# A decoder trunk's two mixers: part of the weight splitting moved from VectorE to GpSimd, one job ahead of its products

## The chip, the cores and the metric

The kernel runs on one core of one Trainium2 chip. The metric is the device time of one execution in microseconds (us); the time before is the median of three runs. The core's engines are called by the names of the profile: PE (TensorE, the matrix products), PEld (its weight loads), DVE (VectorE), ACT (ScalarE), POOL (GpSimd) and SP (SyncE, whose queue issues the loads). Each engine works through its own queue of instructions in a fixed order and waits at an instruction until what that instruction needs is there.

## The reference, cut to what matters

A trunk of two layers on 256 tokens of width 1024. Layer 0 has a hybrid mixer (four heads of a gated delta rule and four heads of block attention, side by side), layer 1 an attention mixer with low-rank queries and keys (MLA). After each mixer comes a feed-forward layer of 16384 single-neuron experts.

```
for layer in range(DEPTH):
    mod = cond @ mod_w[layer] + mod_b[layer]
    sh1, sc1, g1, sh2, sc2, g2 = jnp.split(mod[:, None, :], 6, axis=-1)
    h = rmsnorm(x, norm_mix[layer]) * (1.0 + sc1) + sh1
    if layer % 2 == 0:
        y = hybrid_mixer(h, ...)      # h @ w_in, delta rule and block attention, @ w_out
    else:
        y = mla_mixer(h, ...)         # h @ w_in, @ w_uq, @ w_ukv, attention, @ w_out
    x = x + g1 * y
    h = rmsnorm(x, norm_ffn[layer]) * (1.0 + sc2) + sh2
    x = x + g2 * peer_ffn(h, ...)
return rmsnorm(x, final_norm)
```

In the delta rule, each chunk of 64 tokens needs the inverse of a unit lower triangular matrix, a chain of small products; `o_a = rmsnorm(o_a, o_norm) * silu(z_a)` closes it, and `z_a` is one more part of `h @ w_in`.

## The kernel before, in words

All products are in fp32 accuracy from a faster number form, fp32r: each operand is split into a part `hi` and a rest `lo`, and `mm3` (lines 134 to 138) makes three matrix products of them, hi by hi (L136), hi by lo or lo by hi (L137, L138). `split` (L130 to L132) makes the two parts: the cast to `hi` on ACT, the subtraction of `hi` from the source on DVE. Both appear in the profile under L132.

**Weights in the mixers.** A weight chunk of 128x2048 (1 MB) is loaded into `wraw` (two buffers) and split by `fetch` in two pieces of 128x1024 into `whi` and `wlo` (three buffers each in the hybrid mixer, two in the MLA mixer). `drive` runs over a list of jobs, one for each chunk and block of products. In each of the two halves of a job it emits some of the job's products, then one piece of the split of a chunk that comes one job (MLA) or two jobs (hybrid) later, and then a step of each of the other chains of work: the delta rule's gates, its triangular inverse and its state, the rotary embedding, the attention and the modulation of the next sub-layer (`mod`, L349, two 128x1024 products with a sum on DVE for each 1 MB of its weights).

**What sets the order.** In the mixers a scheduler orders the instructions of each engine by its own estimates of when they are ready; the written order is only its start. So another engine or another duration for one instruction can change where others stand, on PE, DVE, ACT and SP alike. Within the expert layers the order is the written one. GpSimd's own work in the mixers is small: it multiplies two 128x512 tiles (L1169) and one (L1287) in the delta rule, and four 128x256 tiles for `silu(z_a)` (L1357).

**Names near the change.** `wlo_...` are the split chunks, with a running number. In the hybrid mixer the delta rule's gates go through L1051 to L1073 to the products L1069 and L1088; the scaled keys through L1166 and L1168 to L1177 (the triangle `F`), whose last write is the zeroing of a quarter, L1180; L868 are PE transposes of `F`, and the inverse starts from them (L1190, L1200, L1210, L1212). At the mixer's end L1309 and L1310 are the last state products, L1313 to L1325 scale, norm and gate the result `F` on DVE, L875 transposes it on PE, and the products with `w_out` follow. In the MLA mixer `ckT` is the normed latent, from which keys and values are made.

Of the kernel before, what the change touches and what calls it, by code (L numbers as in the profile page):

```python
# [9 lines left out]
F32 = mybir.dt.float32  # L10
# [57 lines left out]
class Trunk:  # L68
# [58 lines left out]
        nc.vector.memset(self.eps, RS * EPS / 4)  # L127


    def split(self, hi, lo, src):  # L130

        return self.nc.scalar.copy(hi, src), self.nc.vector.tensor_sub(lo, src, hi.bitcast(F32))  # L132

    def mm3(self, out, l, r, start, stop):
        mm = self.nc.tensor.matmul
# [647 lines left out]
        self.nc.sync.dma_start(raw[:, :w], src)  # L783
        return raw

    def fetch(self, src, kt, n, pieces=2, raw=None, parts=None):

        w = kt * n
        raw = self.load(src, w) if raw is None else raw
        hi, lo = parts or (self.t(self.wp, [P, WMAX], F32R, tag=t, bufs=self.sets) for t in ("whi", "wlo"))  # L790
        steps = [lambda c=slice(k * w // pieces, (k + 1) * w // pieces): self.split(hi[:, c], lo[:, c], raw[:, c])
                 for k in range(pieces)]
        return Parts(kt, n, [hi[:, :w]], [lo[:, :w]]), steps

    def weights(self, src, kt, n, raw=None):
# [5 lines left out]
    def drive(self, jobs, chains, early=()):  # L801

        self.later = []
        early = list(early)
        ws = []

        def get():  # L810
            if len(ws) < len(jobs):
                w = early.pop(0) if early else None
                ws.append(w if isinstance(w, tuple) else self.fetch(*jobs[len(ws)][0], raw=w))
        ahead = self.sets - 1
        for _ in range(ahead):
            get()
        for w, steps in ws:
            while steps:
                steps.pop(0)()
        for j in range(len(jobs)):  # L820
            get()
            steps = ws[j + ahead][1] if j + ahead < len(jobs) else []
            if len(jobs[j]) > 2:
                jobs[j][2]()
            g = jobs[j][1](ws[j][0])
            for half in range(2):
                late, self.later = self.later, []
                next(g, None)
                if steps:
                    steps.pop(0)()  # L830
                for f in late:
                    f()
                for c in list(chains):
                    if next(c, chains) is chains:
                        chains.remove(c)
            for _ in g:
                pass
            while steps:
                steps.pop(0)()
# [1041 lines left out]
```

## Time and profile before

| | |
|---|---|
| time before, median of 3 runs | 1913.13 us (1910.81 to 1915.3) |
| time of the profiled execution | 1913.58 us |
| its span in the trace | 1911.8 us |
| mean granted TensorE clock | 0.997 of full speed |
| PE busy | 1878.6 us (98%) |
| DVE busy | 1532.3 us (80%) |
| ACT busy | 943.5 us (49%) |
| POOL busy | 48.9 us (3%) |

The hybrid mixer lies at about 45 to 205 us, the MLA mixer at about 995 to 1110 us; the rest is the conditioning at the start and the two expert layers. A row of a timeline gives the start, the duration, the engine, the line, the operation with its tiles, and in brackets how long the engine stood idle before it and which instruction ended that. A matmul's duration overlaps the next one's: what it costs PE is the step from start to start.

### The profile page before, as it was taken

The page shows a single profiled execution, that of the slowest core. Times are in us where ns is not written, and L with a number is a line of the kernel's source. Part 1 is how long each engine was busy: PE and PEld are TensorE (multiplying, and loading weights), DVE is VectorE, ACT ScalarE, POOL GpSimd, SP SyncE. Part 2 cuts the span into 40 slices and gives each one's busy share as a digit, 9 for nine tenths or more (in the row PEclk, how much of TensorE's full clock was granted, in tenths as well). Part 3 has the DMA queues.
Part 4 walks back from the last instruction along what each step waited for, and adds up shares of the span by engine and source line. Part 5 has one row for each costly group of instructions (what it writes and reads, how often), then busy time and mean ns, then how long its engine had stood idle before and what let it go on. Part 6 is the DMA issues. An engine that isn't in the chain of part 4 may idle for free.

```text
span 1911.8 us, 35995 instructions
## 1 busy us (share of the span) xinstructions
PE 1878.6 (98%) x14368; PEld 1722.2 (90%) x14368; DVE 1532.3 (80%) x3265; ACT 943.5 (49%) x1301; POOL 48.9 (3%) x131
## 2 busy tenths in 40 slices
PE   6999999999999999999999999999999999999998
PEld 6999899999999888888889899999999988888886
DVE  7879789999998789865657677999778878985565
ACT  2866555454444444454545754545444444444453
POOL 7001000000000000000000000000000000000000
PEclk9999999999999999999999999999999999999999
DMA  8456475658885555576743455565555555556673
GB/s 324 160 194 214 191 279 187 201 187 284 295 270 187 177 177 177 176 251 195 216 147 111 155 201 175 183 203 186 180 175 170 176 177 176 176 180 199 194 228 103
DMA packets 96504, 374.57 MB, mean 196 GB/s; under 512 B 11856, under 2 KB 12112, under 8 KB 89680
## 3 DMA queue, kind: packets, MB, share of 16 engines
q1 hardware_dynamic: 96336, 372.28, 58.4%
q8 instruction: 112, 1.84, 0.4%
q14 instruction: 56, 0.46, 0.1%
HBM read 371.18 MB, written 1.05 MB: 195 GB/s over the span
## 4 chain that ended last, share of the span: by engine, by line
PE 82%; DVE 9%; DMA 4%; ACT 3%; issue 1%; SPq 0%; ACTq 0%; DVEq 0%
PE ps L776 30%; PE ps L621 21%; PE ps L623 11%; PE ps L136 3%; PE ps L138 3%; PE ps L137 3%; PE ps L644 3%; DVE lo L132 3%; DMA raw<-in_v_dram 2%; PE ps L729 1%; DVE t L349 1%; PE ps L324 1%; ACT hi L132 1%; PE ps L1200 1%; DVE wlo L132 1%
## 5 line engine op out<-in xcount | busy, mean ns | idle before, releaser
L132 ACT CAST hi<-raw 128x1024 fp32r<-128x1024 f32 x508 | 534.8, 1054 | 753.1 <-PE ps L776 310.5
L132 DVE TENSOR_TENSOR lo<-raw,hi 128x1024 fp32r<-128x1024 f32 x508 | 620.0, 1222 | 249.0 <-ACT hi L132 246.8
L621 PE MATMUL ps<-hT,hi 128*128 128x256 f32 x4096 | 514.2, 278 | 0.0
L621 PEld LDWEIGHTS ps<-hT,hi 128*128 128x128 f32 x4096 | 485.8, 188 | 0.2 <-ACT hi L132 0.2
L623 PE MATMUL ps<-hT,lo 128*128 128x256 f32 x2048 | 276.7, 278 | 2.0 <-DVE lo L132 1.9
L776 PE MATMUL ps<-hi,vwh 128*128 128x512 f32 x976 | 266.1, 394 | 1.2 <-ACT hi L132 1.1
L776 PE MATMUL ps<-hi,vwl 128*128 128x512 f32 x976 | 261.3, 389 | 0.0
L776 PE MATMUL ps<-lo,vwh 128*128 128x512 f32 x976 | 260.9, 389 | 0.0
L623 PEld LDWEIGHTS ps<-hT,lo 128*128 128x128 f32 x2048 | 252.4, 188 | 4.1 <-DVE lo L132 3.7
L776 PEld LDWEIGHTS ps<-hi,vwl 128*128 128x128 f32 x976 | 183.2, 188 | 38.8
L776 PEld LDWEIGHTS ps<-lo,vwh 128*128 128x128 f32 x976 | 183.2, 188 | 38.3
L776 PEld LDWEIGHTS ps<-hi,vwh 128*128 128x128 f32 x976 | 180.3, 188 | 38.1 <-ACT hi L132 2.9
L132 DVE TENSOR_TENSOR wlo<-wraw,whi 128x1024 fp32r<-128x1024 f32 (+1 forms) x84 | 99.3, 1202 | 36.1 <-ACT whi L132 36.0
L132 ACT CAST whi<-wraw 128x1024 fp32r<-128x1024 f32 (+1 forms) x84 | 84.3, 1032 | 36.5 <-PE ps L137 14.2
L640 DVE TENSOR_TENSOR ohG<-ohB,t 128x512 f16<-128x512 f16 x256 | 99.3, 418 | 0.0
L136 PE MATMUL ps<-hT,whi 128*128 128x256 f32 x288 | 85.0, 296 | 7.1 <-ACT hT L247 7.1
L634 DVE TENSOR_TENSOR ohA<-t,t 128x1024 f16<-128x1024 f16 x128 | 87.6, 684 | 0.0
L137 PE MATMUL ps<-hT,whi 128*128 128x256 f32 x288 | 83.1, 289 | 0.2 <-DVE hT L251 0.2
L138 PE MATMUL ps<-hT,wlo 128*128 128x256 f32 x288 | 83.1, 289 | 0.0
L644 PE MATMUL ps<-ohG,ohA 128*128 128x64 f16 x2048 | 79.0, 193 | 0.3
L644 PEld LDWEIGHTS <-ohA 128*128 128x128 f16 x2048 | 67.3, 97 | 12.2 <-issue 8.7
L349 DVE SCALAR_TENSOR_TENSOR t<-t,t 128x1024 f32<-128x1024 f32 x56 | 67.4, 1217 | 2.5 <-DMA t<-in_modT_dram 2.5
(478 smaller groups left out, 2251.7 us busy)
## 6 DMA issues: line engine op xcount, KB each, us to landing
raw<-in_uT_dram SPq DMA_DIRECT2D x256, 512.0 KB, 3.3
raw<-in_v_dram SPq DMA_DIRECT2D x256, 512.0 KB, 4.1
t<-in_modT_dram SPq DMA_DIRECT2D x56, 512.0 KB, 5.0
wraw<-in_w_dram SPq DMA_DIRECT2D x13, 1024.0 KB, 6.0
raw<-in_modT_dram SPq DMA_DIRECT2D x24, 512.0 KB, 4.4
wraw<-in_wq_dram SPq DMA_DIRECT2D x12, 1024.0 KB, 5.7
mw<-in_mod_dram SPq DMA_DIRECT2D x8, 1024.0 KB, 13.6
wraw<-in_w0start_dram SPq DMA_DIRECT2D x4, 1024.0 KB, 12.0
```

Of the source, the lines that this page charges most:

```text
L132: return self.nc.scalar.copy(hi, src), self.nc.vector.tensor_sub(lo, src, hi.bitcast(F32))
L136: mm(out, l[0], r[0], start=start, stop=False)
L137: mm(out, l[0], r[1], start=False, stop=False)
L138: mm(out, l[1], r[0], start=False, stop=stop)
L324: mm(ps[g][:, i], e.hT[:, s, k, sl], w[:, b, k, :], start=s + k + b == 0, stop=s == 1 and n == KD - 1)
L349: self.nc.vector.scalar_tensor_tensor(w, w, 1.0, self.row, op0=OP.mult, op1=OP.mult, accum_out=self.modc[layer][:, c:c + 1])
L621: mm(pair, hi[:, k], hT[:, s, k], start=k == 0 and s == 0, stop=False)
L623: mm(pair, lo[:, k], hT[:, 0, k], start=False, stop=k == KD - 1)
L634: nc.vector.tensor_tensor(A, self.iota_t[:, None].to_broadcast(full), pairs(0, full), op=OP.is_equal)
L640: nc.vector.tensor_tensor(B[:, j], b0, pairs(2 + j, part), op=OP.mult)
L644: nc.tensor.matmul(ps[:, t], A[:, t // 2, :, t % 2], B[:, j, t // 2, :, t % 2], start=j == 0, stop=j == 1)
L776: self.nc.tensor.matmul(acc[i][c], w[a][:, j, i * P:(i + 1) * P], v[b][:, c * 512:(c + 1) * 512], start=first and j + a + b == 0, stop=False)
```

## The change

`split` and `fetch` take an engine for the subtraction. `fetch` gives it to the last of its pieces only, and `drive` asks for GpSimd in the chunks that it fetches itself. Chunks that are fetched before `drive`, and the queries' weights, stay wholly on DVE. So 12 chunks of the hybrid mixer and 9 of the MLA mixer have the `lo` part of their second half, 128x1024 each, subtracted on GpSimd: 21 of the 84 subtractions `wlo`. The cast to `whi` stays on ACT.

```diff
-    def split(self, hi, lo, src):
+    def split(self, hi, lo, src, engine=None):
 
-        return self.nc.scalar.copy(hi, src), self.nc.vector.tensor_sub(lo, src, hi.bitcast(F32))
+        return self.nc.scalar.copy(hi, src), (engine or self.nc.vector).tensor_sub(lo, src, hi.bitcast(F32))
...
-    def fetch(self, src, kt, n, pieces=2, raw=None, parts=None):
+    def fetch(self, src, kt, n, pieces=2, raw=None, parts=None, engine=None):
...
-        steps = [lambda c=slice(k * w // pieces, (k + 1) * w // pieces): self.split(hi[:, c], lo[:, c], raw[:, c])
-                 for k in range(pieces)]
+        steps = [lambda c=slice(k * w // pieces, (k + 1) * w // pieces), v=(None, engine)[k == pieces - 1]:
+                 self.split(hi[:, c], lo[:, c], raw[:, c], v) for k in range(pieces)]
...
-                ws.append(w if isinstance(w, tuple) else self.fetch(*jobs[len(ws)][0], raw=w))
+                ws.append(w if isinstance(w, tuple) else self.fetch(*jobs[len(ws)][0], raw=w, engine=self.nc.gpsimd))
```

The scheduler then places the mixers' instructions anew. On GpSimd, at the end of the hybrid mixer, the subtractions come in between the products of `silu(z_a)` (L1357, tile `t_568`) that the result's gate L1325 on DVE needs:

```order
 L1357 TENSOR_TENSOR t_568<-t_568,t_102 128x256
 L1287 TENSOR_TENSOR t_733<-qkv_560,t_733 128x512
-L1357 TENSOR_TENSOR t_568<-t_568,t_102 128x256 x3
+L1357 TENSOR_TENSOR t_568<-t_568,t_102 128x256
+L132 TENSOR_TENSOR wlo_2082<-wraw_2079,whi_2081 128x1024
+L1357 TENSOR_TENSOR t_568<-t_568,t_102 128x256 x2
+L132 TENSOR_TENSOR wlo_2162<-wraw_2159,whi_2161 128x1024
+L132 TENSOR_TENSOR wlo_2196<-wraw_2193,whi_2195 128x1024
```

The third and fourth L1357 now stand behind the second half of `wlo_2082`.

On DVE, where the delta rule's triangle is made (some 80 to 92 us before): the piece from the scaling of the keys (L1166) to the zeroing of the first triangle's quarter (L1180), `F_898`.

```order
 L1166 TENSOR_TENSOR t_730<-t_730,ps_902 128x512
-L922 TENSOR_TENSOR ropf_166_1005<-ps_979,t_100 128x128
+L349 SCALAR_TENSOR_TENSOR raw_1229,t_86<-raw_1229,t_88 128x1024
 L1168 TENSOR_TENSOR k_154_908<-t_730,t_728 128x512
-L923 TENSOR_TENSOR lo_741<-rope_165_1004,ropf_166_1005 128x2x64
+L1166 TENSOR_TENSOR t_731<-t_731,ps_954 128x512
 L1177 SCALAR_TENSOR_TENSOR F_898<-ps_911,t_892,k_154_908 128x128 x4
-L924 TENSOR_TENSOR rope_165_1004<-ps_979,t_100 128x128
-L925 TENSOR_TENSOR ropf_166_1005<-ps_979,t_100 128x128
-L1166 TENSOR_TENSOR t_731<-t_731,ps_954 128x512
-L926 TENSOR_TENSOR lo_741<-rope_165_1004,ropf_166_1005 128x2x64
-L1180 MEMSET F_898 64x4x64
```

Small rotary steps have left the piece and a 128x1024 modulation product (L349) has come in; another L349 comes in just ahead of the piece (behind the step L1149), and a third between the piece and the zeroing of the second triangle. All three stood behind both triangles before.

On PE, at the end of the hybrid mixer, the transposes L875 of the gated result `F_2030` stood before behind the `w_out` products of four accumulators, `ps_2163`, `ps_2178` (not shown), `ps_2197` (not shown) and `ps_2212`:

```order
L138 MATMUL ps_2212<-whi_2081,qkT_1869 128x512
L136 MATMUL ps_2212<-whi_2081,qkT_1869 128x512
L137 MATMUL ps_2212<-wlo_2082,qkT_1869 128x512
L875 MATMUL ps_2145<-t_76,F_2030 128x128 x4
L875 MATMUL ps_2152<-t_76,F_2030 128x128 x4
```

and stand now behind those of the first alone:

```order
L138 MATMUL ps_2163<-whi_1900,qkT_1869 128x512
L136 MATMUL ps_2163<-whi_1900,qkT_1869 128x512
L137 MATMUL ps_2163<-wlo_1901,qkT_1869 128x512
L875 MATMUL ps_2145<-t_76,F_2030 128x128 x4
L138 MATMUL ps_2163<-whi_1900,qkT_1869 128x512
L875 MATMUL ps_2152<-t_76,F_2030 128x128 x4
L136 MATMUL ps_2178<-whi_1900,qkT_1869 128x512
```

L875 has moved ahead of 36 products of 128x512. On DVE the gate L1325 has moved too: it stands now ahead of both first halves of the last two chunks (`wlo_2162`, `wlo_2196`), of which it had three pieces ahead of it.

## Rows read from the trace of the kernel before

**Rows 1.** The page, part 1 (busy time of each engine) and part 4 (the chain).

```profile
PE 1878.6 (98%) x14368; PEld 1722.2 (90%) x14368; DVE 1532.3 (80%) x3265; ACT 943.5 (49%) x1301; POOL 48.9 (3%) x131
...
PE 82%; DVE 9%; DMA 4%; ACT 3%; issue 1%; SPq 0%; ACTq 0%; DVEq 0%
```

**Rows 2.** The page, part 5: the subtractions, the modulation; busy, mean ns | idle before.

```profile
L132 DVE TENSOR_TENSOR wlo<-wraw,whi 128x1024 fp32r<-128x1024 f32 (+1 forms) x84 | 99.3, 1202 | 36.1 <-ACT whi L132 36.0
...
L349 DVE SCALAR_TENSOR_TENSOR t<-t,t 128x1024 f32<-128x1024 f32 x56 | 67.4, 1217 | 2.5 <-DMA t<-in_modT_dram 2.5
```

**Rows 3.** Stretches of 20 us: busy time (instructions) of each engine, PEclk, DMA share.

```profile
50.00:70.00 20.00, 19.26 (x147) 18.36 (x146) 16.98 (x45) 18.35 (x35) 0.00 (x0) 0.88 0.64 222
70.00:90.00 20.00, 19.90 (x163) 19.52 (x163) 16.77 (x59) 13.40 (x26) 2.58 (x2) 0.95 0.43 147
...
190.00:210.00 20.00, 19.36 (x94) 15.17 (x93) 17.76 (x46) 7.58 (x21) 0.77 (x17) 1.00 0.55 209
...
1020.00:1040.00 20.00, 18.90 (x158) 18.18 (x157) 17.08 (x58) 12.31 (x24) 0.00 (x0) 1.00 0.59 209
```

**Rows 4.** Timeline of POOL in the hybrid mixer: start, duration, [idle before <-releaser].

```profile
83.07 1.28 POOL L1169 TENSOR_TENSOR t<-t,t 128x512 f32<-128x512 f32 x1 [35.15 <-issue]
...
168.59 0.74 POOL L1357 TENSOR_TENSOR t<-t,t 128x256 f32<-128x256 f32 x1 [79.63 <-ACT t L1356]
170.48 1.46 POOL L1287 TENSOR_TENSOR t<-qkv,t 128x512 f32<-128x512 f32 x1 [1.15 <-ACT qkv L1116]
...
181.30 1.10 POOL L1357 TENSOR_TENSOR t<-t,t 128x256 f32<-128x256 f32 x1 [5.52 <-ACT t L1356]
```

**Rows 5.** Timeline of DVE beside those POOL instructions.

```profile
170.73 2.29 DVE L349 SCALAR_TENSOR_TENSOR raw<-raw,t 128x1024 f32<-128x1024 f32 x1
...
176.87 0.15 DVE L182 TENSOR_TENSOR rs_4t<-rs_4t,rs_4v 128x8 f32<-128x8 f32 x1
...
181.74 0.68 DVE L182 TENSOR_TENSOR rs_4t<-rs_4t,rs_4v 128x8 f32<-128x8 f32 x1
```

**Rows 6.** Timeline of DVE, from the gates to the second triangle's end.

```profile
76.51 0.17 DVE L1071 COPY t<-ps 128x8 f32<-128x8 f32 x1 [0.56 <-PE ps L1069]
...
91.60 0.27 DVE L1180 MEMSET F<- 64x256 f32 x1 [0.59 <-ACT t L1179]
```

**Rows 7.** Timeline of PE: the second triangle's transposes, and two products at full clock.

```profile
71.95 0.28 PE L136 MATMUL ps<-whi,hT 128*128 128x256 f32 x1
72.07 0.28 PE L137 MATMUL ps<-wlo,hT 128*128 128x256 f32 x1
...
91.93 0.66 PE L868 MATMUL ps<-t,F 128*128 128x128 f32 x4
```

**Rows 8.** Timeline of PE, end of the hybrid mixer.

```profile
179.35 0.39 PE L1310 MATMUL ps<-k,F 128*128 128x128 f32 x2
...
193.83 0.39 PE L136 MATMUL ps<-whi,qkT 128*128 128x512 f32 x1
194.06 0.39 PE L137 MATMUL ps<-wlo,qkT 128*128 128x512 f32 x1
194.93 1.23 PE L875 MATMUL ps<-t,F 128*128 128x128 f32 x8 [0.48 <-DVE F L1325]
```

**Rows 9.** Timeline of DVE there.

```profile
194.10 1.29 DVE L1325 TENSOR_TENSOR F<-F,t 128x512 f32<-128x512 f32 x2
```

**Rows 10.** Timeline of PE: the wait that precedes the slow clock.

```profile
64.57 0.28 PE L1035 MATMUL ps<-t,k 8*128 8x8 f32 x2 [0.74 <-ACT k L1031]
```

**Rows 11.** Timeline of PE, DVE and ACT, each apart, in the MLA mixer.

```profile
1032.69 0.51 PE L136 MATMUL ps<-ckT,whi 128*128 128x256 f32 x2 [0.82 <-ACT ckT L132]
...
1102.80 0.39 PE L137 MATMUL ps<-wlo,qn 128*128 128x512 f32 x1
...
1026.98 1.22 DVE L132 TENSOR_TENSOR wlo<-wraw,whi 128x1024 fp32r<-128x1024 f32 x1
...
1098.56 2.00 ACT L132 CAST whi<-wraw 128x1024 fp32r<-128x1024 f32 x2 [2.16 <-PE ps L138]
```

## The prediction

> **What bounds the kernel now.** I read the busy times and the chain first. PE is busy for 1878.6 us of the 1911.8, and the chain of work that ended last is PE for 82% and DVE for 9% [rows 1]. So PE sets the time, and DVE counts only where PE stands waiting for it. Next I read the stretches of the two mixers, since nothing else changes its order. In the hybrid mixer PE is busy for 19.90 of 20 us at 70 to 90 us and for 19.36 of 20 at 190 to 210 us; the worst stretch of the MLA mixer has 18.90 of 20 [rows 3]. DVE is busy for 16.8 to 17.8 us of those same stretches, close to PE but below it. The reader is to see two things here. There is little to win: idle PE in the stretches shown, past the one at 50 to 70 us where no moved subtraction runs yet, sums to 0.10 + 0.64 + 1.10 us. And PE has almost no slack anywhere: whatever comes later than PE's fixed order expects is paid in full.
>
> **What is removed.** 21 subtractions of 1.20 us each leave DVE [rows 2], 25 us in all, 12 in the hybrid mixer (14.4 us) and 9 in the MLA mixer (10.8 us). None of this is on PE's path except at the waits for DVE named below. So removing it is worth at most those waits.
>
> **What is added.** GpSimd gets the same 21. The trace has no 128x1024 subtraction on it. The nearest rows are 0.74 us for 128x256 and 1.28 us for 128x512 [rows 4], that is 0.54 us for 256 more elements, so I take 1.28 + 2 x 0.54 = 2.4 us; from below 1.8 us (half that slope beyond 512 elements, 1.28 + 0.54), from above 2.9 us (twice the 1.46 of L1287). GpSimd itself has room, 48.9 us of work in 1911.8 [rows 1]. What counts is what it does to DVE. While GpSimd's L1287 ran from 170.48 for 1.46 us, DVE's L349 that started at 170.73 took 2.29 us [rows 4, 5] instead of its mean of 1.22 [rows 2]; it ended 1.07 us late, about what GpSimd still had to do (to 171.94). An L182 of 128x8 took 0.68 us beside GpSimd's L1357 at 181.30, which ended at 182.40, instead of 0.15 [rows 4, 5]. Both have two operands in SBUF. So a moved subtraction takes 1.2 us off DVE, and can stop DVE for up to 2.4 us when DVE comes to such an operation meanwhile. Subtractions `wlo`, L349, L1168, L1321 and L1325 are all of this kind. If about half the moved ones meet one near their start, DVE gains nothing on average. The Trainium skill (SBUF — State Buffer, Who interferes with whom) speaks against the change here: a DVE instruction with two SBUF inputs contends with a GpSimd instruction that reads SBUF, and the one that issues first holds the shared ports for its whole duration. The trace agrees, with 1.07 us lost by one L349 [rows 4, 5]; without the rule I would put the sum below about 1 us lower.
>
> **What is moved: the triangles (70 to 95 us).** In the new order L868 of the second triangle stands behind 10 products of 128x256 fewer, which step at 0.12 us [rows 7]: PE comes to it 1.2 us earlier. On DVE between L1071 and the second L1180, 15.1 us before [rows 6], three L349 come in (3 x 1.22 = 3.7 us) and one second half `wlo` goes out (1.2). Two convolution steps, three rotary steps net and some small ones go out as well; by their size against L349 I put these at 2 us. That is 0.5 us more, of which DVE's own waits there (0.59 us at its end alone [rows 6]) can take up as much, so -1 to +0.7. Two GpSimd subtractions and two L1169 lie in the stretch; a lock on one of the three L349 costs up to 2.4 us, on two 4.8. PE's stall is 1.2 + (-1 to +0.7) + (0 to 4.8): 0.2 to 6.7 us. I take 1.8, the case of one short lock, as in the row seen (1.07), with DVE's waits taking up part.
>
> **The end (180 to 200 us).** Before, L875 waited 0.48 us for L1325 [rows 8], and the products behind it a few tenths more: 0.8 us that may vanish. Now L875 stands ahead of 36 products of 128x512, 36 x 0.23 = 8.3 us earlier [rows 8]. Between the last L1310 and L875 there stand 40 products of 128x256 and 11 of 128x512: 40 x 0.12 + 11 x 0.23 = 7.3 us. DVE needs, from the first L1313: four pairs of 128x512 (L1313, L1316, L1321, L1325) of 1.29 us [rows 9], three pieces `dead` at 0.65 (half of such a pair) and nine small operations of 0.15 to 0.2 us: 5.2 + 2.0 + 1.6 = 8.8 us. It can begin about 1 us after L1310, since a first half `wlo_2082` and one `dead` still stand ahead. That is 9.8 us against 7.3, a stall of 2.5 us; by 1.5 us less, if DVE has run ahead through its relief, and up to 5 us more, if the second half of `wlo_2082` on GpSimd (2.4 us) and the two L1357 behind it hold L1321 or L1325. I take 2.6 - 0.8 = 1.8 us, bounds 0.2 to 6.7.
>
> **The rest of the hybrid mixer.** The gates at 70 to 77 us are small operations with two SBUF inputs under the first two GpSimd subtractions; I take 0.3 us (0 to 2). Between 95 and 165 us the modulation moved forward leaves DVE less to do, and PE is held there by nothing of DVE's: 0, up to 1.
>
> **The MLA mixer.** PE waited 0.82 us for `ckT` [rows 11]. One second half `wlo`, 1.22 us at 1026.98, stood on DVE ahead of it and now goes; GpSimd takes it up beside small operations. I take -0.7 us (-1.1 to +0.5). At the end, the last chunk's `whi` is cast by 1100.56 [rows 11]; GpSimd's 2.4 us then end at 1103.0, while the first product of that half with `wlo` starts at 1102.80 [rows 11]: +0.2 us (0 to 0.8). That is -0.5 in all. `wraw` comes free about 1 us later for each chunk and SP's queue, with the modulation loads behind it, waits for GpSimd too; no row of this mixer or the hybrid one shows PE waiting for a load of weights near its end, so nothing.
>
> **The sum.** 1.8 + 1.8 + 0.3 - 0.5 = +3.4 us. On the profiled execution's own time, 1913.58 us (1.8 us outside its span), it gives 1917.0 us. That execution is 0.45 us above the median of the runs, so I forecast 1916.5 us.
>
> **Rivals.** *The cover holds.* The scheduler put L875 and the triangles earlier by its own reckoning; if DVE really is ahead by the five to six subtractions moved before each place, the stalls stay under 0.5 us each and the waits of 0.8 and 0.7 us go. That gives -1.5 to +1.5 us, 1911.6 to 1914.6. For it: DVE's 16.8 of 20 us [rows 3] leave room for a delay to be caught up. Against it: the order on PE moved forward by more than one subtraction is worth.
>
> *The lock, with the clock.* In the row at 64.57 PE waited 0.74 us behind tiny products [rows 10], and the granted clock was 0.88 over 50 to 70 us and 0.95 over 70 to 90 us [rows 3], the lower of the two levels (1.2 GHz) for part of it. This cost 20 x 0.12 + 20 x 0.05 = 3.4 us. The clock did not fall at the MLA mixer's 0.82 us wait, where it stayed 1.00 [rows 3, 11]. The place where this can come again is L875 at the end: if GpSimd's `wlo_2082` and the L1357 behind it hold L1325, the stall is 5 us instead of 2.5. [...] The sum is then 3.4 + 2.5 + 3.4 = +9.3, 1922.4 us (1920 to 1926).
>
> *Faster.* All waits of PE for DVE vanish and the new order stalls nowhere: 0.8 + 0.7 us and the tenths at L868 give -2 us, not over 0.2%. To exceed 3.8 us the slow stretch at 65 us would have to end sooner, but it comes before the first moved subtraction. A price of 1907 to 1911 us, mostly by chance of the clock.
>
> *The change does nothing.* GpSimd's subtractions could end later than their products in general. But the pieces are split one or two jobs ahead, and a job of the hybrid mixer takes about 9 us (18 jobs in some 160 us); only the last chunk of the MLA mixer is near, as priced.
>
> **How the numbers follow.** The measurement of this kernel can tell about 0.2%, 3.8 us, from no change: below 1909.3 is faster, above 1917.0 slower. The forecast's case (1914.6 to 1920) gets 0.50, nearly half of it above 1917.0; the cover holds 0.30; the lock with the clock 0.14; faster 0.06. So slower 0.24 + 0.14 = 0.38, faster 0.05, same 0.57. The range from 1911.2 to 1923.0 takes in the first two cases and most of the third.
>
> **What would show it.** The subtractions on GpSimd at 2.2 to 2.6 us; DVE operations with two SBUF inputs (L349, L1168, L1321) of 2 us and more beside them; PE waiting 1 us or more at L868 for L1180 and at L875 for L1325; 0.5 us or less at `ckT`. It is wrong if the GpSimd subtraction takes 1.8 us or less, if PE's waits at L868 and L875 together stay under 1 us, or if PE loses time at a place not named, such as the inverse's products (L1200, L1210) or a load.

## The result and the profile after

The changed kernel takes 1931.66 us (median of 4 runs, 1929.1 to 1933.32) beside 1912.26 us for the kernel before on the same chip: a ratio of 1.0098 with a 95% interval of 1.0081 to 1.0116, slower by about 19 us. The forecast was 1916.5 us, with a range up to 1923.0. The profiled execution took 1931.4 us, its span 1929.6, 17.8 us more than before.

The first lines to set against [rows 1] are the busy times of the page of the changed kernel:

```profile
PE 1881.3 (97%) x14368; PEld 1723.6 (89%) x14368; DVE 1535.6 (80%) x3244; ACT 942.9 (49%) x1301; POOL 104.3 (5%) x152
```

DVE has 21 instructions fewer, which had taken 21 x 1.20 = 25.2 us [rows 2], and yet it is busy for 3.3 us more. So the instructions that stayed on DVE take some 28 us longer than they did. PE does the same 14368 products with 2.7 us more of busy time; the other 15.1 of the 17.8 us are idle time of PE. The first product of the first expert layer (L621) starts at 275.4 us instead of 263.9: 11.5 us are lost by the end of the hybrid mixer, and the other 6.3 us in the MLA mixer. The stretches of the changed kernel, in the columns of [rows 3], show where:

```profile
50.00:70.00 20.00, 19.34 (x142) 18.44 (x141) 17.21 (x45) 17.77 (x33) 0.54 (x1) 0.85 0.68 238
70.00:90.00 20.00, 16.30 (x135) 15.79 (x134) 19.41 (x50) 10.99 (x22) 9.50 (x5) 0.98 0.52 185
...
190.00:210.00 20.00, 15.62 (x66) 12.58 (x65) 14.74 (x23) 5.43 (x7) 5.79 (x3) 0.91 0.44 168
...
1060.00:1080.00 20.00, 18.04 (x133) 17.31 (x132) 8.90 (x15) 12.63 (x24) 4.87 (x2) 0.91 0.35 131
```

At 70 to 90 us PE falls from 19.90 to 16.30 us while DVE rises from 16.77 to 19.41: DVE is now the one that is waited for. At 190 to 210 us PE has 15.62 instead of 19.36 us. The granted clock has a new dip there (0.91, before 1.00), and another at 1060 to 1080 us. Before, the same stretch of time had the full clock:

```profile
1060.00:1080.00 20.00, 19.34 (x146) 18.10 (x145) 11.23 (x20) 15.27 (x40) 0.00 (x0) 1.00 0.35 131
```

Most of the cause stands in the timelines of POOL and DVE, here at four places of the changed kernel (start, duration; POOL's row first, then DVE's):

```profile
69.46 2.73 POOL L132 TENSOR_TENSOR wlo<-wraw,whi 128x1024 fp32r<-128x1024 f32 x1 [19.60 <-ACT whi L132]
...
85.40 2.38 POOL L132 TENSOR_TENSOR wlo<-wraw,whi 128x1024 fp32r<-128x1024 f32 x1 [0.32 <-ACT whi L132]
...
192.49 2.58 POOL L132 TENSOR_TENSOR wlo<-wraw,whi 128x1024 fp32r<-128x1024 f32 x1 [1.17 <-ACT whi L132]
...
1063.81 2.50 POOL L132 TENSOR_TENSOR wlo<-wraw,whi 128x1024 fp32r<-128x1024 f32 x1 [6.85 <-ACT whi L132]
...
69.86 2.35 DVE L1058 TENSOR_TENSOR t<-t,t 128x8 f32<-128x8 f32 x1
...
85.60 2.73 DVE L1168 TENSOR_TENSOR k<-t,t 128x512 f32<-128x512 f32 x1
...
192.18 3.44 DVE L1321 TENSOR_TENSOR F<-F,t 128x512 f32<-128x512 f32 x2
...
1064.01 2.44 DVE L926 TENSOR_TENSOR qr<-rope,ropf 128x128 f32<-128x128 f32 x1
```

The subtraction takes 2.4 to 2.7 us on GpSimd. L1058 works on 128x8 elements; [rows 5] has 0.15 us for another operation of that size. It starts 0.40 us after GpSimd and ends at 72.21, GpSimd at 72.19. L1168, of 128x512 elements, would take half of the pair in [rows 9], some 0.65 us; it ends at 88.33, 0.55 us after GpSimd's end at 87.78: it began its work when GpSimd had ended. The pair L1321 takes 3.44 us instead of the 1.29 of the like pair in [rows 9]. By comparing each DVE instruction beside a GpSimd subtraction with the usual duration of its form, 17 of the 21 subtractions stop one DVE instruction each, for 0.3 to 2.2 us, 26.7 us in all. The other four stop none: beside them DVE is idle (one), takes no second operand from SBUF (two), or had started first (one, where GpSimd took 2.94 us).

PE's waits of the changed kernel that answer to [rows 7, 8, 11], and those at new places:

```profile
80.01 0.41 PE L1164 MATMUL ps<-t,t 128*128 128x128 f32 x2 [1.84 <-DVE t L1149]
...
88.86 0.52 PE L868 MATMUL ps<-t,F 128*128 128x128 f32 x3 [1.76 <-DVE F L1180]
...
163.55 0.38 PE L1277 MATMUL ps<-k,k 128*128 128x128 f32 x1 [1.48 <-ACT k L1272]
...
196.28 0.66 PE L875 MATMUL ps<-t,F 128*128 128x128 f32 x4 [4.38 <-DVE F L1325]
...
199.07 0.63 PE L136 MATMUL ps<-whi,qkT 128*128 128x512 f32 x1
199.50 0.63 PE L137 MATMUL ps<-wlo,qkT 128*128 128x512 f32 x1
...
1040.94 0.30 PE L1464 MATMUL ps<-t,lat 128*128 128x128 f32 x1 [0.96 <-DVE lat L1458]
...
1066.51 0.55 PE L868 MATMUL ps<-t,qr 128*128 128x128 f32 x3 [1.96 <-DVE qr L926]
...
1100.99 0.33 PE L868 MATMUL ps<-t,att_s 128*128 128x128 f32 x1 [1.73 <-ACT att_s L949]
```

These seven waits sum to 14.1 us. The last of them, for `att_s`, is not made by a stop of DVE, since the two subtractions ahead of it (1083.00 and 1090.25) stop nothing there. The rows of POOL, SP and ACT ahead of it, and last the cast on ACT as it was before:

```profile
1090.25 2.35 POOL L132 TENSOR_TENSOR wlo<-wraw,whi 128x1024 fp32r<-128x1024 f32 x1 [4.88 <-ACT whi L132]
...
1092.62 0.33 SPq L783 DMA_DIRECT2D wraw<-in_w1out_dram  x1
...
1099.39 1.04 ACT L132 CAST hi<-raw 128x1024 fp32r<-128x1024 f32 x1 [2.36 <-DMA raw<-in_wq_dram]
1100.34 0.50 ACT L949 ACTIVATE att_s<-att_s,att_c 128x256 f32<-128x256 f32 x1
...
1082.72 1.05 ACT L132 CAST hi<-raw 128x1024 fp32r<-128x1024 f32 x1 [1.26 <-DMA raw<-in_wq_dram]
```

The subtraction reads `wraw` until 1092.60. Only then can SP issue the next load into this buffer (1092.62), and the load of the expert layer's weights `raw` stands behind it in SP's queue. ACT waits for that load 2.36 us at its cast, before 1.26, and the `att_s` that PE needs stands behind the cast in ACT's queue. After the longest wait, products of 128x512 step at 0.43 us instead of 0.23 [rows 8]: the lower of the two levels of the clock (1.2 GHz). By the stretches, 20 x 0.09 us at 190 to 210 us and as much at 1060 to 1080 us are lost that way, 3.6 us in all.

### The profile page after: what moved, and what is told of

Same layout as the page of the kernel before. It is cut to its first block, busy times and chain, and to the rows that moved or that the text cites. A ratio compares the mean times of both kernels' runs of the same rounds, so it can differ in the third digit from the quotient of the medians.

```text
span 1929.6 us, 36051 instructions
## 1 busy us (share of the span) xinstructions
PE 1881.3 (97%) x14368; PEld 1723.6 (89%) x14368; DVE 1535.6 (80%) x3244; ACT 942.9 (49%) x1301; POOL 104.3 (5%) x152
## 3 DMA queue, kind: packets, MB, share of 16 engines
q8 instruction: 112, 1.84, 0.4%
## 4 chain that ended last, share of the span: by engine, by line
PE 80%; DVE 10%; DMA 4%; ACT 3%; issue 2%; SPq 0%; POOL 0%; ACTq 0%; DVEq 0%; POOLq 0%
PE ps L776 31%; PE ps L621 21%; PE ps L623 11%; PE ps L644 3%; PE ps L137 3%; PE ps L136 3%; PE ps L138 3%; DVE lo L132 2%; DMA raw<-in_v_dram 2%; PE ps L729 1%; DVE t L349 1%; PE ps L324 1%; ACT hi L132 1%; PE ps L1200 1%; DMA raw<-in_wq_dram 1%
## 5 line engine op out<-in xcount | busy, mean ns | idle before, releaser
L621 PE MATMUL ps<-hT,hi 128*128 128x256 f32 x4096 | 513.3, 278 | 0.0
L621 PEld LDWEIGHTS ps<-hT,hi 128*128 128x128 f32 x4096 | 484.9, 188 | 0.1
L132 DVE TENSOR_TENSOR wlo<-wraw,whi 128x1024 fp32r<-128x1024 f32 (+1 forms) x63 | 78.3, 1263 | 35.4 <-ACT whi L132 35.2
L137 PE MATMUL ps<-hT,whi 128*128 128x256 f32 x288 | 83.1, 289 | 0.0
L349 DVE SCALAR_TENSOR_TENSOR t<-t,t 128x1024 f32<-128x1024 f32 x56 | 67.4, 1219 | 2.3 <-DMA t<-in_modT_dram 2.3
```

Of the source, the lines that this page charges most:

```text
L132: return self.nc.scalar.copy(hi, src), (engine or self.nc.vector).tensor_sub(lo, src, hi.bitcast(F32))
L137: mm(out, l[0], r[1], start=False, stop=False)
L349: self.nc.vector.scalar_tensor_tensor(w, w, 1.0, self.row, op0=OP.mult, op1=OP.mult, accum_out=self.modc[layer][:, c:c + 1])
L621: mm(pair, hi[:, k], hT[:, s, k], start=k == 0 and s == 0, stop=False)
```

## The experiments

For the larger part of the loss, two reasons remained open after this look. The new order on all engines might bring PE to DVE's results too early ("order"), or GpSimd's subtractions might stop DVE in any order ("lock"). The two could be taken apart, since the two kernels issue the same instructions, but for the engine of 21 of them. In e1 and e2 a table of the other kernel's order, where the two differ, is laid over a kernel as edges between neighbours that set the order of issue and add no wait:

```diff
+QUEUES = [
+    ("PE", """984 985 986 987 988 989 990 991 992 993 720 721 778 779 780 781 790 791 792 793 994 995 996 997 998 999 1000
...
+def follow(tc, nc):
+    traced = {i.name: i for i in nc.cur_bb.bb.instructions}
+    info = mybir.DependencyInfo(mybir.DependencyClass.NoSync, mybir.DependencyReason.DATA)
+    for _, numbers in QUEUES:
+        names = [f"I-{n}" for n in numbers.split()]
+        for a, b in zip(names, names[1:]):
+            tc.add_manual_dep(traced[b], a, info, reason="order")
...
         trunk(tc, aps, out)
+        follow(tc, nc)
```

**e1, the old order with GpSimd.** The changed kernel, with the tables of the kernel before for PE, DVE, ACT and SP.

> The 21 subtractions are on GpSimd as in the changed kernel, but on PE, DVE, ACT and SP everything else stands in the order of the kernel before. Theory 'order' (the scheduler's new order brings PE to DVE's results too early, and that makes the 19 us): 1912 to 1916 us. Theory 'lock' (DVE is stopped by the GpSimd subtractions, in any order): 1922 to 1932 us. If both must come together, something between, 1916 to 1922 us.

Measured 1931.12 us, ratio 1.0092 (1.0071 to 1.0114), the same as the changed kernel. So the new order isn't needed for the loss. The longest waits of PE in e1's mixers (the summary of waits: waited for, us in total, times, longest):

```profile
PE ps L875 <- DVE F L1325: 5.1, 1, 5.1
...
PE ps L137 <- DVE wlo L132: 2.2, 2, 1.4
...
PE ps L868 <- DVE qr L926: 1.9, 1, 1.9
...
PE ps L138 <- POOL wlo L132: 1.3, 1, 1.3
PE ps L868 <- DVE F L1180: 1.2, 1, 1.2
PE ps L868 <- ACT att_s L949: 1.2, 1, 1.2
```

L875 stands here where it stood before, behind the 36 products that the new order puts after it, and its wait is longer (5.14 us, in the changed kernel 4.38). DVE is as late in the old order. The smaller waits change with the order: L1164 and L1277 are not among those of e1, while PE waits 2.2 us for `wlo` at L137. The low clock behind L875 lasts longer than in the changed kernel:

```profile
190.00:210.00 20.00, 14.86 (x60) 12.14 (x59) 17.61 (x30) 6.41 (x11) 5.36 (x3) 0.83 0.58 215
```

**e2, the new order without GpSimd.** The kernel before, with the tables of the changed kernel.

> All subtractions are on DVE as in the kernel before, but PE, DVE, ACT and SP have the order of the changed kernel; the 21 subtractions stand on DVE close behind their casts. Theory 'order': 1924 to 1934 us, PE waiting 1 us and more at L1164, L868 and L875 again. Theory 'lock': 1912 to 1917 us.

Measured 1922.69 us, ratio 1.0051 (1.0036 to 1.0066): neither theory's number. The new order was made for a DVE with 25 us less to do; with this work put back on DVE, PE waits at the two places where the prediction put the loss, L868 and L875, and at L1464 of the MLA mixer (the three longest in the mixers, again from the summary of waits):

```profile
PE ps L868 <- DVE F L1180: 1.9, 2, 1.0
PE ps L875 <- DVE F L1325: 1.8, 1, 1.8
...
PE ps L1464 <- ACT whi L132: 1.3, 1, 1.3
```

**e3 and e4, GpSimd writes but doesn't read.** The half chunk is filled with zeros on GpSimd, behind the same cast; e3 has the new order, e4 the old.

```diff
-        return self.nc.scalar.copy(hi, src), (engine or self.nc.vector).tensor_sub(lo, src, hi.bitcast(F32))
+        return (c := self.nc.scalar.copy(hi, src)), cleared(self, c, lo, engine) if engine else self.nc.vector.tensor_sub(lo, src, hi.bitcast(F32))
...
+def cleared(k, cast, lo, engine):
+    zero = engine.memset(lo.bitcast(F32), 0.0)
+    info = mybir.DependencyInfo(mybir.DependencyClass.Sync, mybir.DependencyReason.DATA)
+    k.tc.add_manual_dep(zero.ins, cast.ins.name, info, reason="as the subtraction")
+    return zero
```

> The changed kernel's order, and GpSimd fills the same half of each chunk's lo part with zeros, behind the same cast, instead of subtracting: it writes but reads nothing, and the products then lack the lo part of these halves. DVE keeps its relief of 25 us and is not stopped. Theory 'order': 1922 to 1930 us. Theory 'lock': 1909 to 1914 us.

> As the one before (GpSimd writes zeros, reads nothing, the lo part of these halves is left out), in the order of the kernel before: what DVE's relief is worth by itself. Both theories: 1909 to 1913 us, since PE waits for DVE only some 2 to 3 us in the two mixers. If it were below 1909, the relief alone would have been worth a change.

Measured 1912.9 us for e3, ratio 0.9997 (0.9986 to 1.0009), and 1910.62 us for e4, ratio 0.9987 (0.9974 to 1.0000). With DVE relieved and not stopped, both orders cost nothing that can be told from no change, and the relief by itself is worth 0.26% at the very most. So in these two orders, taking the 21 subtractions off DVE can't win more than some 5 us, and about 2 us is likely. In the new order PE's wait at L1164 is there without any stop, so most of the changed kernel's 1.84 us there belongs to the order (e3):

```profile
76.10 0.62 PE L1164 MATMUL ps<-t,t 128*128 128x128 f32 x4 [1.38 <-DVE t L1149]
```

DVE's busy time in e4 is the measure for the others, since its list of instructions on DVE is that of e1:

```profile
PE 1872.8 (98%) x14368; PEld 1717.5 (90%) x14368; DVE 1509.7 (79%) x3244; ACT 943.0 (49%) x1301; POOL 71.9 (4%) x152
```

The same line of e1 has 1539.4 us for DVE: 29.7 us more for the same instructions.

**e5, writes only, but as long.** The writes of e4 take 0.95 us each, the subtraction 2.5. So e5 writes the half two and a half times over (the edit against e4).

```diff
     k.tc.add_manual_dep(zero.ins, cast.ins.name, info, reason="as the subtraction")
-    return zero
+    engine.memset(lo.bitcast(F32), 0.0)
+    return engine.memset(lo[:, :512].bitcast(F32), 0.0)
```

> As e1 (order of the kernel before), but GpSimd writes zeros into the half for about as long as the subtraction took, two and a half times over (0.95 us for 128x1024, so about 2.4 us), and reads nothing; the products lack the lo part of these halves. Theory 'lock by reading': DVE isn't stopped, 1909 to 1914 us. Theory 'length' (the lo part comes 1.3 us later and the load buffer is freed later, and that makes the loss): 1922 to 1932 us.

Measured 1914.12 us, ratio 0.9999 (0.9989 to 1.0008). The three groups of GpSimd's instructions that make the 2.4 us (count, then busy time and mean ns of one):

```profile
L1867 POOL MEMSET wlo<- 128x1024 f32 x21 | 20.1, 956 | 182.7 <-ACT whi L132 162.8 <-DVE lo L926 19.9
L1870 POOL MEMSET wlo<- 128x1024 f32 x21 | 20.0, 954 | 1.1
L1871 POOL MEMSET wlo<- 128x512 f32 x21 | 11.1, 528 | 1.2
```

They sum to 51 us, near the 52.5 us of the 21 subtractions, and DVE's busy time (1511.3 us) is only 1.6 above e4's. PE does wait 2.2 us for late `wlo` in e5, but its time is that of the kernel before. That the lo part comes later isn't the cause of the 19 us; that GpSimd reads is. Reading does two things, though: it stops DVE, and it keeps `wraw` occupied to the end of the subtraction, which a write doesn't. The wait for `att_s` tells the second apart: PE has 1.2 us of it or more in every run whose GpSimd instructions in the MLA mixer read `wraw` (e1, e6, e7, e8, e9: 1.2 to 2.0 us), and none in e3, e4 and e5.

**e6, one operand read.** GpSimd multiplies the loaded chunk by zero into the half (the edit against e4).

```diff
-    zero = engine.memset(lo.bitcast(F32), 0.0)
+    zero = engine.tensor_scalar(lo, src, 0.0, None, op0=OP.mult)
```

> As e1, but GpSimd reads one operand (the loaded chunk, times zero) instead of two; the products lack the lo part of these halves. If any read of GpSimd stops DVE's operations with two inputs from SBUF, and the operation takes 1.5 to 2.5 us: 1918 to 1931 us, with single DVE operations 1 to 2 us longer than before. If only an operation with two reads does: 1909 to 1914 us.

Measured 1920.82 us, ratio 1.0037 (1.0027 to 1.0048). DVE's busy time is 1518.0 us, 8.3 above e4's. The time is in the range of the first case, but the sign named for it, single operations 1 to 2 us longer, is not there: the operation is longer than the subtraction (2.77 us at the least), and yet the stops are short. The place of L1058 in e6, POOL's row and DVE's:

```profile
69.97 3.11 POOL L1867 TENSOR_SCALAR wlo<-wraw 128x1024 fp32r<-128x1024 f32 x1 [20.20 <-ACT whi L132]
...
70.36 1.00 DVE L1058 TENSOR_TENSOR t<-t,t 128x8 f32<-128x8 f32 x1
71.29 0.28 DVE L926 TENSOR_TENSOR lo<-rope,ropf 128x128 f32<-128x128 f32 x1
```

L1058 ends at 71.36, 1.4 us after GpSimd's start and 1.7 us before its end, and L926, with two SBUF operands too, then runs undisturbed beside it. Seven of the ten stops over 0.25 us in e6 are of 0.82 to 0.86 us, and none is longer. So part of e6's loss is of another kind: PE waits 2.6 us for `wlo` that comes later still, and 2.0 us for `att_s` behind the late load.

**e7, four pieces.** The subtraction in four GpSimd instructions of 128x256, in the old order.

```diff
+def quarters(lo, src, hi, engine):
+    for q in range(4):
+        s = slice(256 * q, 256 * q + 256)
+        last = engine.tensor_sub(lo[:, s], src[:, s], hi[:, s].bitcast(F32))
+    return last
```

> As e1, but each GpSimd subtraction is made in four pieces of 128x256 (0.74 us each by the trace of before). Theory 'lock for one instruction': a DVE operation is stopped for at most one piece, and the sum lost on DVE falls from 30 us to about half: 1917 to 1925 us. If DVE is held until all four pieces are through, or if each piece costs GpSimd and DVE more than its share: 1928 to 1936 us.

Measured 1924.35 us, ratio 1.0048 (1.0032 to 1.0065), half of e1's loss; DVE's busy time is 1525.5 us, 15.8 above e4's, half of 29.7. One place of it, POOL's four pieces and two DVE instructions with two SBUF operands beside them:

```profile
106.28 2.84 POOL L1869 TENSOR_TENSOR wlo<-wraw,whi 128x256 fp32r<-128x256 f32 x4 [11.71 <-ACT whi L132]
...
106.32 0.83 DVE L923 TENSOR_TENSOR lo<-rope,ropf 128x128 f32<-128x128 f32 x1
...
108.42 0.84 DVE L926 TENSOR_TENSOR lo<-rope,ropf 128x128 f32<-128x128 f32 x1
```

Each waits about 0.55 us, for the rest of one piece. A piece takes 0.91 us on the mean instead of the 0.74 of [rows 4]; I take the difference for GpSimd's own waits for DVE, which was not tested. The four pieces keep `wraw` no shorter than the one subtraction did (PE waits 1.6 us for `att_s`), so the half that was won back comes by the shorter stops of DVE.

**e9, the end of the hybrid mixer on DVE.** As e1, but four chunks stay on DVE.

```diff
-                ws.append(w if isinstance(w, tuple) else self.fetch(*jobs[len(ws)][0], raw=w, engine=self.nc.gpsimd))
+                ws.append(w if isinstance(w, tuple) else self.fetch(*jobs[len(ws)][0], raw=w, engine=None if self.sets == 3 and len(ws) > 13 else self.nc.gpsimd))
```

> As e1, but the last four chunks of the hybrid mixer (those for the output projection) are wholly on DVE again, where they stood before; 17 subtractions stay on GpSimd. In e1 PE waited 5.1 us at L875. If the stops by these four make that wait: 1923 to 1927 us. If DVE is late there because of what came earlier in the mixer: 1928 to 1932 us.

Measured 1925.36 us, ratio 1.0056 (1.0039 to 1.0073). PE's wait at L875 falls from 5.14 us to that of [rows 8]:

```profile
199.52 0.63 PE L875 MATMUL ps<-t,F 128*128 128x128 f32 x4 [0.51 <-DVE F L1325]
```

The stops by these four alone made it.

**e8, the MLA mixer alone.** As e1, with `engine=(None, self.nc.gpsimd)[self.sets == 2]`.

> Order of the kernel before; only the 9 subtractions of the MLA mixer are on GpSimd, the 12 of the hybrid mixer are on DVE where they stood. By the places at which PE waited in e1, the MLA mixer has about 4 of its 15 us in the trace: 1916 to 1919 us. If the hybrid mixer's stops make the later loss too (a shared cause such as the clock), 1912 to 1915 us; if the MLA mixer carries as much as the hybrid one, 1921 to 1925 us.

Measured 1918.88 us, ratio 1.0030 (1.0018 to 1.0043): 5.7 us from 9 subtractions, at the upper end of the first number. If the two mixers' losses add, about 12 of e1's 17.6 us are the hybrid mixer's. The trace of e1 divides its loss in much the same way: L621 starts 10.0 us later than before, and the other 5.1 us come behind it.

The runs side by side, with DVE's busy time above e4's where the DVE instructions are the same:

| run | order | GpSimd's work for a half chunk | DVE above e4, us | ratio |
|---|---|---|---|---|
| e4 | old | writes, 0.95 us | 0 | 0.9987 |
| e5 | old | writes, 2.4 us | 1.6 | 0.9999 |
| e6 | old | reads one, 2.9 us | 8.3 | 1.0037 |
| e7 | old | reads two, 4 x 0.91 us | 15.8 | 1.0048 |
| e1 | old | reads two, 2.5 us | 29.7 | 1.0092 |
| e3 | new | writes | 0 | 0.9997 |
| changed | new | reads two, 2.5 us | 25.9 | 1.0098 |

## Why the prediction was wrong

The sign, the mechanism on DVE and the duration on GpSimd (2.4 us forecast, 2.5 measured on the mean) were right. The step that failed is the one from DVE to PE: where PE pays for the stops. By the traces, the hybrid mixer cost 11.5 us where the terms of the sum give 1.8 + 1.8 + 0.3 = 3.9, and the MLA mixer 6.3 us where they give -0.5.

**How often DVE is stopped.** The prediction has "if about half the moved ones meet one near their start, DVE gains nothing on average". As a sum on DVE this came out nearly right, but by luck: no row stands behind the half. A stop needs only one such operation to come up at any time within the 2.4 us, and DVE issues several instructions in that time. So 17 of 21 subtractions met one, for 1.6 us on the mean, and these 26.7 us are little more than the 25.2 us taken off. The Trainium skill (SBUF — State Buffer, Who interferes with whom) has the rule that I put at about 1 us of the sum: the engine that issues first holds the shared ports for the whole instruction. The subtraction agrees (L1058 ended 0.02 us after GpSimd), and e5 against e1 shows what GpSimd's reading was worth, stops and held buffer together: some 18 us by their ratios.

**Where the stops fall.** That DVE gains nothing doesn't mean that PE loses nothing. The 25 us taken off DVE were not on PE's path, and the prediction said so. The stops are of another kind: DVE's operations with two SBUF inputs are the links of chains that PE waits for (L1168 and L1180 for L868, L349 and L1112 for L1277, L1321 and L1325 for L875, L926 for the attention). The prediction priced this in full only at the two places where the new order had moved PE. By place, forecast and measured: the gates 0.3, and 1.84 us at L1164, inside the bound of 2, of which e3 has 1.38 without a stop; the triangles 1.8, and 1.76 us at L868; the middle 0, bound 1, and 1.48 us at L1277; the end 2.6 before what vanishes, and 4.38 us at L875, inside its bound.

**The MLA mixer.** Forecast -0.5 us, bounds -1.1 to about +1.3; e8 measures +5.7 in the old order. I had looked only at the waits of PE for DVE that the trace of before has, and at the last chunk. Of the new waits, 1.96 us at L868 for the rotary part L926 and 0.96 us at L1464 are at operations that a stop made late, and the stretch at 1060 to 1080 us has the low clock.

**The load buffer.** The prediction saw that `wraw` comes free about 1 us later and that SP's queue waits for GpSimd, and put it at "so nothing", since no row showed PE waiting for a load. The load counts by way of ACT: before, ACT already waited 1.26 us for it, and PE behind that 0.19 us for `att_s`. Set against PE's products L343 close by, SP issues the load of `wraw` 1.2 us later in the changed kernel (0.61 us after them) than before (0.60 us ahead of them), and PE's wait is 1.73 us.

**The order.** The prediction rested the stalls at L868 and L875 on PE coming earlier by 1.2 and 8.3 us. e1 has the old order and the same time, e3 the new order and no loss. Only with all subtractions back on DVE (e2) does the new order cost time, about 10 us. The rows of order told where instructions stood, but not what made DVE late.

**The clock.** The rival of the lock with the clock was the nearest, at 1922.4 us and a chance of 0.14; its two steps, a stall of 5 us at L875 and the low clock behind it, are what the trace shows (4.38 us, 1.8 us by the stretch), though L1321 was stopped by the subtraction after the one that it named. What it lacked are the MLA mixer, the waits at L1164 and L1277, and a second dip. The rival that the cover holds came true only for kernels whose GpSimd doesn't read (e3, e5).

What stays open: in e1 the clock takes 20 x 0.17 = 3.4 us of the 17.6 by the stretch at 190 to 210 us, but no run holds the clock up, and none gives `wraw` free early while GpSimd reads. So the shares of the stops, the clock and the load are read from waits and not from runs of their own.

## What to carry to other kernels

Before moving work from DVE to GpSimd, ask what DVE does in any stretch as long as the GpSimd instruction: if one operation with two inputs from SBUF comes up in it, DVE loses the rest of the stretch, and the chain that this operation belongs to loses it too. Ask also which buffer the moved instruction reads, and which load waits for that buffer. Price the relief first, by a version in which the moved work is left out or only written: here it was worth at most 0.26%, so little could have been won. Where such a move is wanted all the same, shorter GpSimd instructions lose less (here four in place of one halved the loss), and chunks whose subtraction falls beside a chain that PE waits for (the last four of the hybrid mixer, 0.36% of the time between e1 and e9) belong on DVE.

## What the runs showed of the hardware that was not expected

A GpSimd instruction with two SBUF inputs stopped a DVE operation with two such inputs to its own end (L1058, of 128x8, was 2.2 us late); one with a single input, although longer, stopped it for at most 0.86 us, after which operations with two inputs ran beside it (e6), and one that only writes stopped it hardly at all: with 63 writes, DVE was busy for 1.6 us more than with 21 (e5, e4). A DVE operation with a single SBUF input was stopped too: a 128x8 `tensor_scalar`, L1073, started at 75.78 in the changed kernel and took 2.33 us beside the subtraction at 75.72:

```profile
75.72 2.36 POOL L132 TENSOR_TENSOR wlo<-wraw,whi 128x1024 fp32r<-128x1024 f32 x1 [3.54 <-DVE t L1071]
...
75.78 2.33 DVE L1073 TENSOR_SCALAR t<-t 128x8 f32<-128x8 f32 x1
```

The Trainium skill (SBUF — State Buffer, Who interferes with whom) counts `tensor_scalar` among the operations that can take the shared ports, which agrees with this row; for the single read of e6, which the skill would have hold the ports for its whole instruction, the measurement decides.
